# A decoder layer's down projection: where VectorE's queue has the weight sums of steps two and three of a block product, against the residual sums of the product before

## The chip, the cores and the metric

The kernel runs on one core of a Trainium2 chip, in one launch. The metric is device time in microseconds, as the median of several runs. TensorE (PE in the profile) multiplies, VectorE (DVE) and ScalarE (ACT) do the elementwise work, GpSimd (POOL) a few small powers, and SyncE (SP) issues all loads and stores. Each engine works through its own queue in a fixed order, and waits at an instruction whose input isn't there yet.

## The reference

One layer of a decoder trunk on x of 1024 tokens by 1024, all in float32: RMSNorm, one input projection, gated DeltaNet and dilated attention side by side, output projection, residual; then RMSNorm, an up projection to 2 x 2816 columns, a causal convolution of width 3, SiLU gate, the down projection, residual and a last RMSNorm. The part that matters here:

```python
    x = x + jnp.concatenate([o_a, o_b], axis=-1) @ w_out
    h = rmsnorm(x, norm2_w)
    u = causal_dwconv(h @ w_up, ffn_conv_w)
    gate, up = u[..., :D_FF], u[..., D_FF:]
    x = x + (jax.nn.silu(gate) * up) @ w_down          # 2816 -> 1024
    return rmsnorm(x, final_norm_w)
```

## The kernel before

Everything is held transposed: features on the 128 partitions, tokens along the free dimension. A float32 product is made of three fast ones (`mm3`, line 196): each operand is split into a hi part, a rounded copy that ScalarE makes, and a lo part, source minus hi, that VectorE makes (`split_block`, line 1138); the products are hi by hi, hi by lo and lo by hi, in this order.

The down projection (`mlp_down`, line 1452) is a block scheme with seven products instead of eight: the 1024 outputs are halved (512 each, four tiles of 128), the 1024 tokens are halved, and the 2816 inputs are halved (11 tiles of 128 each). It has four stages. Stages 0, 1 and 2 make two block products at a time, one in the four PSUM banks `pa`, one in the four banks `pb`; stage 3 makes one. I call what a stage makes its product. Each stage runs over 11 steps j, called (stage, j) below. A step has, for each of the eight banks, three products of 128 by 128 by 512, so 24.

For a step, `prep` (line 1365) loads the weights (`wd`, `wa`) and activations (`r`, `q`, from the parking place `upark`) and makes the combinations that the scheme needs, on VectorE. In stage 1 these are two weight sums, 512 wide (lines 1381 and 1382), and differences of activations (`t2`, and `r` in place); in stage 2 a weight difference, 1024 wide (1391), a weight sum, 512 wide (1392), and a difference of activations. Then everything is split into hi and lo (`pr` tiles). The weight tiles turn in tags of two buffers each (`wst`, `whi`), so the load of step j + 2 has to wait until step j's tile was last read, which is the lo part of its split.

When a stage's last step (j = 10) is through, `add_to` (line 1415) adds each bank to the residual tiles `x1h` on VectorE: eight residual sums a stage, four for `pa` and four for `pb`. The next stage's first products write the same eight banks in the same order, and each has to wait for its bank's sum. After stage 0's second four, `complete` (1419) also squares the rows on ScalarE and adds the squares on VectorE (`rstdB`).

The residual tiles come from memory by `load_x1` (line 1401): eight loads of 256 KB stand at steps (1,1) and (1,3) of the loop.

What sets the order: TensorE's order is that of the program, held by a token (line 189). In the program's order, the preparation of a step stands ahead of the products of the step before it. The order on the other queues is worked out by the framework's scheduler at build time, from a simulated timeline, so it may put a weight sum of a later step ahead of residual sums that the program has earlier. `after(inst, anchor)` (line 185) is a dependency without a semaphore: the scheduler must put `inst` behind `anchor` in the same queue, and nothing is waited for.

In the order before, the first two weight sums of (1,1) and of (1,2) stand ahead of all eight residual sums of stage 0; among the residual sums stand the lo parts of (1,1). In the same way the difference and sum of (2,1) and the difference of (2,2) stand ahead of all residual sums of stage 1.

Of the kernel before, what the change touches and what calls it, by code (L numbers as in the profile page):

```python
# [10 lines left out]
OP = mybir.AluOpType  # L11
# [133 lines left out]
def hybrid_layer(tc, I, out):  # L145
    nc = tc.nc
    wv = Weave()
    ve = Engine(wv, nc.vector, "vector", 0.07, 0.00105)
# [14 lines left out]
    def tile_(pool, shape, dt, name, tag, bufs):  # L163
        return wv.slot(pool.tile(list(shape), dt, name=name, tag=tag, bufs=bufs), tag, bufs)
# [3 lines left out]
    def A(name, tag, dt=F32, shape=(P, 1024)):  # L168
        if tag in TURNS:
            i = turns[tag] = turns.get(tag, -1) + 1  # L170
            tag = TURNS[tag][i % len(TURNS[tag])]
        return tile_(lp, shape, dt, name, tag, SLOTS[tag])
# [12 lines left out]
    def after(inst, anchor, reason="keeps a slot free until it is needed"):  # L185
        tc.add_manual_dep(inst.ins, anchor.ins.name, order, reason=reason)
# [66 lines left out]
    def half(i):  # L253
        return slice(i * 512, i * 512 + 512)
# [17 lines left out]
    for k in range(KT):  # L272
# [30 lines left out]
        else:  # L303
            inst = ve.tensor_tensor(acc, acc, sq, op=OP.add)
# [1002 lines left out]
    def mlp_up():  # L1307
        yield from wv.until("last weights")
        yield from wv.until("proj")
        up_weights(0, ("A12", "S2", "A22", "S3", "S4"))  # L1310
        rest = None
        for n in range(FT):
            if n + 1 < FT:
                load_up(n + 1)
            yield from up(n, rest)
            rest = last["rest"]
            if n + 1 < FT:
                up_weights(n + 1, UORDER)
        prep(0, 0)
        yield from rest()  # L1320
        wv.done.add("up")
# [12 lines left out]
    def raw_tile(name, tag, src, n=2):  # L1334
        t = tile_(wp, [P, n, 512], F32, name, tag, 2)
        sy.dma_start(t, src)
        return t

    def wd_rows(j, mg):
        v = I["wd"].rearrange("(e j p) c -> j p e c", e=2, p=P)  # L1340
        return v[j, :, :, mg * 512:mg * 512 + 512]

    def acts(name, tag, j, hh):
        t = A(name, tag, shape=(P, 2, 512))
        sy.dma_start(t, upark.rearrange("(e j) p t -> j p e t", e=2)[j, :, :, half(hh)])
        return t

    def split_pair(src):
        hi, lo = [], []
        for d in (hi, lo):  # L1350
            d.append(A("pr", PTAGS[pcount[0] % len(PTAGS)], F32R, (P, 2, 512)))
            pcount[0] += 1
        split_block((hi[0], lo[0]), src)
        return [(hi[0][:, i, :], lo[0][:, i, :]) for i in range(2)]

    def split_one(src, tag=None):
        if tag is None:
            tag = PTAGS[pcount[0] % len(PTAGS)]
            pcount[0] += 1
        t = A("pr", tag, F32R, (P, 2, 512))  # L1360
        b = t[:, 0, :], t[:, 1, :]
        split_block(b, src)
        return b

    def prep(stage, j):
        if stage == 0:

            g = raw_tile("wd", ("wst", "whi")[j % 2], wd_rows(j, 0))
            r = R1[j] = acts("r1", R1TAGS[j], j, 0)
            ops[stage, j] = list(zip(split_pair(g), split_pair(r)))  # L1370
            q = R2[j] = A("r2", R2TAGS[j], shape=(P, 2, 512))
            sy.dma_start(q[:, 0, :], upark[j][:, half(1)])
            ve.tensor_tensor(r[:, 0, :], q[:, 0, :], r[:, 0, :], op=OP.subtract)
        elif stage == 1:

            u = raw_tile("wd", "wst", wd_rows(j, 1))
            a = raw_tile("wa", "whi", wd_rows(j, 0)[:, 0:1], 1)
            r, q = R1[j], R2[j]
            sy.dma_start(q[:, 1, :], upark[HT + j][:, half(1)])
            t2 = tile_(wp, [P, 512], F32, "t2", "wlo", 2)  # L1380
            ve.tensor_tensor(u[:, 1, :], u[:, 0, :], u[:, 1, :], op=OP.add)
            ve.tensor_tensor(u[:, 0, :], u[:, 1, :], a[:, 0, :], op=OP.subtract)
            ve.tensor_tensor(t2, q[:, 1, :], r[:, 0, :], op=OP.subtract)
            w = split_pair(u)
            ops[stage, j] = [(w[0], split_one(t2)), (w[1], split_one(r[:, 0, :]))]
            ve.tensor_tensor(r[:, 1, :], r[:, 1, :], t2, op=OP.subtract)
        elif stage == 2:

            g = raw_tile("wd", "wst", wd_rows(j, 0))
            u = raw_tile("wd", "whi", wd_rows(j, 1))  # L1390
            ve.tensor_tensor(g, g, u, op=OP.subtract)
            ve.tensor_tensor(g[:, 1, :], g[:, 0, :], g[:, 1, :], op=OP.add)
            r = R2[j]
            ve.tensor_tensor(r[:, 0, :], r[:, 1, :], r[:, 0, :], op=OP.subtract)
            ops[stage, j] = list(zip(split_pair(g), split_pair(r)))
        else:

            a = raw_tile("wa", ("wst", "whi")[j % 2], wd_rows(j, 1)[:, 1:2], 1)
            ops[stage, j] = [(split_one(a[:, 0, :]), split_one(R1[j][:, 1, :], R2TAGS[j]))]
# [12 lines left out]
    def part(m, hh, sl):  # L1412
        return slice(512 * hh + sl.start, 512 * hh + sl.stop)

    def add_to(pd, m, hh, sl):
        x = x1h[m][:, part(m, hh, sl)]
        ve.tensor_tensor(x, x, pd[:, sl], op=OP.add)

    def complete(m, hh, sl):

# [31 lines left out]
    def mlp_down():  # L1452
# [4 lines left out]
        def down_step(stage, j):  # L1457
            for e, (op, pds) in enumerate(zip(ops[stage, j], (pa, pb))):
                for i in range(4):
                    down(pds[i], i, op, whole, j == 0 and (stage == 0 or (stage, e) == (1, 1)), j == HT - 1)  # L1460
                if j == HT - 1:
                    mg, hh = ADDS[stage][e]
                    for i in range(4):
                        add_to(pds[i], 4 * mg + i, hh, whole)
                        if stage == 0 and e == 1:
                            complete(i, 0, whole)
                        if stage == 2 and e == 1:
                            complete(i, 1, whole)
                    if stage == 2 and e == 1:
                        for i in range(4):  # L1470
                            complete(4 + i, 1, whole)

        for n, (stage, j) in enumerate(STEPS):
            if n + 1 < len(STEPS):
                prep(*STEPS[n + 1])
            if n in XLOADS:
                load_x1(*XLOADS[n])
            if stage == 3 and j == HT - LAST - 1:
                final_norm(1, whole, ("hf", "ch"), lambda: down_step(stage, j))
            elif stage < 3 or j < HT - LAST:  # L1480
                down_step(stage, j)

        def last_product(i, sl):
            for j in range(HT - LAST, HT):
                down(pa[i], i, ops[3, j][0], sl, False, j == HT - 1)
            add_to(pa[i], 4 + i, 0, sl)
            complete(4 + i, 0, sl)
# [82 lines left out]
```

## Time and profile before

| what | us |
|---|---|
| median of 3 runs | 1223.47 |
| lowest and highest of them | 1223.26, 1225.77 |
| the profiled execution, its own time | 1226.47 |
| its span, first to last instruction | 1224.7 |
| down projection, first product to last residual sum | about 995 to 1206 |

The profile is of one execution. Its times count from the start of the span. A row of an engine's order of time has start, duration, engine, line, operation, what is written and read, the count of merged instructions, and in brackets the idle time before it with what ended it. Since a helper records each operation, nearly all rows have line 139 or 189, and the tile's name tells them apart: `dw` are the eight banks, `x1h<-x1h,dw` a residual sum, `wd<-wd` or `wd<-wd,wa` a weight sum, `pr<-wd`, `pr<-t`, `pr<-r` a hi part on ACT and a lo part on DVE.

### The profile page before, as it was taken

The numbers are of one execution on the slowest core, as the hardware profiler recorded it, in microseconds if no ns is written. First come the engines' busy times: TensorE is split into PE (matmuls) and PEld (weight loads), VectorE is DVE, ScalarE is ACT, GpSimd is POOL, SyncE is SP. The second block draws the span as 40 slices with busy tenths as digits, with TensorE's granted clock in tenths as the row PEclk, the third lists the DMA queues.
The fourth block names the chain that finished last, engine by engine and source line by source line (L and its number), as shares of the span: only waits on it lengthen the run. The fifth ranks groups of instructions, "written<-read, shape, count | busy, mean of one in ns | idle before, by whom it ended". The sixth has DMA issues, their size and how long they took to land.

```text
span 1224.7 us, 18240 instructions
## 1 busy us (share of the span) xinstructions
PE 1203.8 (98%) x7064; PEld 988.3 (81%) x7064; DVE 949.1 (77%) x1458; ACT 574.5 (47%) x1123; POOL 52.1 (4%) x46
## 2 busy tenths in 40 slices
PE   9999999999999999999999999999999999999996
PEld 7878887888777778788788888888888888787886
DVE  7675964566477686767888988889888889899975
ACT  7393344356344453655544444445444544344441
POOL 0211010003100000000000000000000000000000
PEclk9999999999999999999999999999999999999999
DMA  7425252345634213444223122131231497455623
GB/s 231 105 81 161 86 143 82 121 131 154 224 103 123 79 36 118 151 153 138 68 71 103 53 102 89 67 104 59 97 97 59 137 370 240 163 164 175 196 86 138
DMA packets 85800, 154.81 MB, mean 126 GB/s; under 512 B 21169, under 2 KB 36305, under 8 KB 85713
## 3 DMA queue, kind: packets, MB, share of 16 engines
q1 hardware_dynamic: 85712, 153.64, 39.1%
q8 instruction: 55, 0.90, 0.3%
q14 instruction: 33, 0.26, 0.1%
HBM read 117.68 MB, written 35.93 MB: 125 GB/s over the span
## 4 chain that ended last, share of the span: by engine, by line
PE 82%; DVE 7%; DMA 6%; issue 2%; ACT 2%; SPq 0%; POOLq 0%; POOL 0%; DVEq 0%; ACTq 0%
PE ps L189 43%; PE pa L189 19%; PE pc L189 9%; PE dw L189 8%; DMA wd<-in_wd 3%; PE ps L193 3%; DMA r<-upark 2%; DVE pr L139 2%; DVE x1h L139 1%; DVE kT L139 1%; DVE wd L139 1%; PE warm L189 1%; ACT dec L139 1%; DVE wlo L139 0%; DMA wst<-in_wu 0%
## 5 line engine op out<-in xcount | busy, mean ns | idle before, releaser
L189 PE MATMUL dw<-pr 128*128 128x512 f32 (+1 forms) x984 | 213.5, 377 | 3.9 <-DVE x1h L139 3.6
L189 PEld LDWEIGHTS dw<-pr 128*128 128x128 f32 x984 | 176.0, 188 | 40.2 <-DVE x1h L139 4.9
L189 PE MATMUL ps<-xhi,whi 128*128 128x512 f32 x384 | 158.6, 413 | 0.0
L189 PE MATMUL ps<-xhi,wlo 128*128 128x512 f32 x384 | 150.2, 391 | 0.0
L189 PE MATMUL ps<-xlo,whi 128*128 128x512 f32 x384 | 150.0, 391 | 0.0
L189 PE MATMUL pa<-T,pair 128*128 128x512 f32 x528 | 128.7, 393 | 1.2 <-ACT u L139 1.2
L189 PEld LDWEIGHTS pa<-T,pair 128*128 128x128 f32 x528 | 100.1, 190 | 22.4 <-ACT u L139 1.5
L189 PEld LDWEIGHTS ps<-xhi,wlo 128*128 128x128 f32 x384 | 72.1, 188 | 15.7
L189 PEld LDWEIGHTS ps<-xhi,whi 128*128 128x128 f32 x384 | 72.3, 188 | 14.9 <-issue 1.4
L189 PEld LDWEIGHTS ps<-xlo,whi 128*128 128x128 f32 x384 | 72.4, 189 | 11.7
L139 ACT ACTIVATE whi<-wst 128x1024 fp32r<-128x1024 f32 (+2 forms) x42 | 43.0, 1023 | 78.3 <-PE ps L189 64.3
L139 ACT ACTIVATE u<-pa 128x512 f32<-128x512 f32 x44 | 26.3, 598 | 110.7 <-PE pa L189 110.7
L139 DVE SCALAR_TENSOR_TENSOR y<-xu,fcw,y 128x1023 f32<-128x1023 f32 (+1 forms) x44 | 56.3, 1281 | 25.7 <-ACT y L139 25.6
L189 PE MATMUL pc<-B,pair 128*128 128x512 f32 x264 | 63.4, 389 | 0.0
L189 PE MATMUL pa<-B,A 128*128 128x512 f32 x264 | 63.4, 389 | 0.0
L189 PE MATMUL pc<-T,S 128*128 128x512 f32 x264 | 63.4, 389 | 0.0
L189 PE MATMUL pa<-T,S 128*128 128x512 f32 x264 | 63.4, 389 | 0.0
L139 DVE TENSOR_TENSOR wst<-wst 128x512 f32<-128x512 f32 x88 | 60.4, 686 | 0.8
L139 ACT ACTIVATE pr<-wd 128x1024 fp32r<-128x1024 f32 x33 | 34.9, 1059 | 55.1 <-DVE wd L139 35.4
L189 PE MATMUL ps<-B,pair 128*128 128x512 f32 x252 | 60.5, 389 | 0.0
L139 DVE TENSOR_TENSOR wlo<-wst,whi 128x1024 fp32r<-128x1024 f32 (+2 forms) x42 | 49.4, 1177 | 13.8 <-ACT whi L139 13.6
L189 PEld LDWEIGHTS pa<-B,A 128*128 128x128 f32 x264 | 49.6, 188 | 10.3
(240 smaller groups left out, 2343.0 us busy)
## 6 DMA issues: line engine op xcount, KB each, us to landing
wst<-in_wu SPq DMA_DIRECT2D x44, 512.0 KB, 3.7
wd<-in_wd SPq DMA_DIRECT2D x44, 512.0 KB, 4.2
upark<-y SPq DMA_DIRECT2D x22, 512.0 KB, 3.7
wst<-in_wi SPq DMA_DIRECT2D x21, 512.0 KB, 3.7
r<-upark SPq DMA_DIRECT2D x11, 512.0 KB, 8.0
r<-upark SPq DMA_DIRECT2D x22, 256.0 KB, 6.8
wa<-in_wd SPq DMA_DIRECT2D x22, 256.0 KB, 2.8
wst<-in_wv SPq DMA_DIRECT2D x8, 512.0 KB, 3.6
```

Of the source, the lines that this page charges most:

```text
L139: return getattr(eng, op)(*a, **kw)
L189: tc.stamp_issue_order_token(nc.tensor.matmul(dst, lhs, rhs, start=start, stop=stop, **kw).ins, TOKEN)
L193: tc.stamp_issue_order_token(nc.tensor.transpose(dst, src, ident if idt is None else idt).ins, TOKEN)
```

## The change

The weight sums of four steps are put behind certain residual sums of the stage before. The residual sums are collected in a list as they are made, eight a stage. The two weight sums of step (1,1) come behind the fourth residual sum of stage 0, those of (1,2) behind the sixth; those of (2,1) behind the second of stage 1, those of (2,2) behind the sixth. Nothing else is edited; the scheduler then works out all queues anew, so VectorE's, ScalarE's and SyncE's orders differ through the rest of the down projection. TensorE's and GpSimd's are the same.

```diff
+    added = []
+    BEHIND = {(1, 1): 3, (1, 2): 5, (2, 1): 1, (2, 2): 5}
+
+    def behind(stage, j, insts):
+        if (stage, j) in BEHIND:
+            for inst in insts:
+                after(inst, added[8 * (stage - 1) + BEHIND[stage, j]], "the banks of the stage are added first")
+
     def prep(stage, j):
...
-            ve.tensor_tensor(u[:, 1, :], u[:, 0, :], u[:, 1, :], op=OP.add)
-            ve.tensor_tensor(u[:, 0, :], u[:, 1, :], a[:, 0, :], op=OP.subtract)
+            behind(stage, j, [ve.tensor_tensor(u[:, 1, :], u[:, 0, :], u[:, 1, :], op=OP.add),
+                              ve.tensor_tensor(u[:, 0, :], u[:, 1, :], a[:, 0, :], op=OP.subtract)])
...
-            ve.tensor_tensor(g, g, u, op=OP.subtract)
-            ve.tensor_tensor(g[:, 1, :], g[:, 0, :], g[:, 1, :], op=OP.add)
+            behind(stage, j, [ve.tensor_tensor(g, g, u, op=OP.subtract),
+                              ve.tensor_tensor(g[:, 1, :], g[:, 0, :], g[:, 1, :], op=OP.add)])
...
     def add_to(pd, m, hh, sl):
         x = x1h[m][:, part(m, hh, sl)]
-        ve.tensor_tensor(x, x, pd[:, sl], op=OP.add)
+        added.append(ve.tensor_tensor(x, x, pd[:, sl], op=OP.add))
```

## The prediction

> **What bounds the kernel now.** I read the page first, then a table of stretches around the down projection, then TensorE's order of time there, and then what VectorE, ScalarE and the loads did at the stops.
>
> ```profile
> span 1224.7 us, 18240 instructions
> PE 1203.8 (98%) x7064; PEld 988.3 (81%) x7064; DVE 949.1 (77%) x1458; ACT 574.5 (47%) x1123; POOL 52.1 (4%) x46
> PE 82%; DVE 7%; DMA 6%; issue 2%; ACT 2%; SPq 0%; POOLq 0%; POOL 0%; DVEq 0%; ACTq 0%
> wd<-in_wd SPq DMA_DIRECT2D x44, 512.0 KB, 4.2
> ```
>
> TensorE has work for 98% of the span and carries 82% of the chain that ended last: only time in which it stands still can be won. The stretches (us, then busy us of PE, PEld, DVE, ACT, POOL, granted clock, DMA share, GB/s) show where that is:
>
> ```profile
> 1052.00:1063.00 11.00, 9.91 (x41) 7.23 (x41) 10.86 (x17) 4.30 (x7) 0.00 (x0) 1.00 0.56 178
> 1063.00:1115.00 52.00, 52.00 (x232) 43.02 (x231) 46.32 (x66) 20.34 (x28) 0.00 (x0) 1.00 0.56 180
> 1115.00:1126.00 11.00, 8.47 (x35) 6.10 (x34) 11.00 (x16) 4.64 (x5) 0.00 (x0) 1.00 0.47 147
> 1205.00:1225.00 20.00, 9.40 (x75) 8.69 (x73) 11.41 (x30) 2.26 (x6) 1.39 (x2) 0.84 0.38 127
> ```
>
> The two short stretches are the passages from product 0 to 1 and from 1 to 2. There VectorE is full and TensorE is not; in between TensorE never stops. TensorE's own order of time gives the stops:
>
> ```profile
> 978.60 2.72 PE pa L189 x12
> 1011.80 44.95 PE L189 MATMUL dw<-pr 128*128 128x512 f32 x197 [0.25 <-DVE pr L139]
> 1057.02 0.96 PE L189 MATMUL dw<-pr 128*128 128x512 f32 x3 [0.27 <-DVE x1h L139]
> 1058.22 3.01 PE L189 MATMUL dw<-pr 128*128 128x512 f32 x12 [0.24 <-DVE x1h L139]
> 1061.82 8.46 PE L189 MATMUL dw<-pr 128*128 128x512 f32 x36 [0.59 <-DVE x1h L139]
> 1069.66 47.53 PE L189 MATMUL dw<-pr 128*128 128x512 f32 x209
> 1118.09 2.33 PE L189 MATMUL dw<-pr 128*128 128x512 f32 x9 [0.89 <-DVE x1h L139]
> 1121.53 3.00 PE L189 MATMUL dw<-pr 128*128 128x512 f32 x12 [1.11 <-DVE x1h L139]
> 1125.05 68.98 PE L189 MATMUL dw<-pr 128*128 128x512 f32 x303 [0.53 <-DVE x1h L139]
> L189 PE MATMUL dw<-pr 128*128 128x512 f32 x864 | 198.4, 390 | 3.9 <-DVE x1h L139 3.6 <-DVE pr L139 0.2
> ```
>
> All six stops are ended by residual sums (x1h). The printed idle times are too small: twelve products take 2.72 (0.227 each), but a product is drawn 0.39 long, so the next could start 0.16 before the printed end. From start to start: the first run ends at 1056.75, the next product could start at 1056.59 and starts at 1057.02 (0.43); three products later 1057.70, started 1058.22 (0.52); twelve later 1060.94, started 1061.82 (0.88): **1.83** lost. In the same way 1117.03 to 1118.09 (1.06), 1120.13 to 1121.53 (1.40), 1124.25 to 1125.05 (0.80): **3.26**. Together 5.1 us, 0.42% of the span, is all that there is to win.
>
> What VectorE does at the first passage, with ScalarE's hi parts and SyncE's loads:
>
> ```profile
> 1049.77 0.63 ACT L139 ACTIVATE pr<-r 128x512 fp32r<-128x512 f32 x1 [3.86 <-PE dw L189]
> 1050.31 1.04 ACT L139 ACTIVATE pr<-wd 128x1024 fp32r<-128x1024 f32 x1
> 1052.14 0.69 DVE L139 TENSOR_TENSOR wd<-wd 128x512 f32<-128x512 f32 x1 [2.23 <-DMA wd<-in_wd]
> 1053.96 1.28 DVE L139 TENSOR_TENSOR x1h<-x1h,dw 128x512 f32<-128x512 f32 x2
> 1055.15 1.22 DVE L139 TENSOR_TENSOR pr<-wd,pr 128x1024 fp32r<-128x1024 f32 x1
> 1056.29 0.68 DVE L139 TENSOR_TENSOR x1h<-x1h,dw 128x512 f32<-128x512 f32 x1
> 1056.40 0.38 SPq L139 DMA_DIRECT2D wd<-in_wd  x1
> 1056.87 4.28 SPq L139 DMA_DIRECT2D x1h<-xpark  x8
> 1057.49 2.47 DVE L139 TENSOR_TENSOR x1h<-x1h,dw 128x512 f32<-128x512 f32 x4
> 1061.68 1.21 DVE L139 TENSOR_TENSOR pr<-wd,pr 128x1024 fp32r<-128x1024 f32 x1
> 1071.47 0.68 DVE L139 TENSOR_TENSOR pr<-t,pr 128x512 fp32r<-128x512 f32 x1
> ```
>
> Four sums take 2.47, so one takes 0.60 of the queue (the last is drawn 0.68); a 1024-wide one 1.14 (1055.15 to 1056.29). The first weight sum of step (1,2) waits 2.23 for its load, and the residual sums wait behind it although the banks are ready: product 1 begins at 1056.59 - 2 x 0.68 = 1055.23 (the two sums at 1053.96 had freed two banks, the third, at 1056.29, ended the stop), so the ended product's first bank was complete 7 x 0.68 earlier, at 1050.5 (1050.6 with the 0.16).
>
> **The change, part by part.** No instruction is added or removed. In the changed program VectorE's order at passage 0-1 is: four residual sums, first weight sum of (1,1), two residual sums, first sum of (1,2), second sum of (1,1), two residual sums, second sum of (1,2), then the lo parts. At 1-2: two residual sums, difference (2,1), a lo part, two, sum (2,1), two, difference (2,2), two, lo parts.
>
> **Stops that go at passage 0-1.** The lo part ahead of the sums needs ScalarE's hi part (1049.77 + 0.63), so it runs at 1050.4; residual sums from 1051.0 at 0.60, each behind its bank, weight sums between: the eighth is done at 1057.7. TensorE wants that bank at 1055.23 + 7 x 0.68 = 1060.0. All 1.83 goes, with 2.3 to spare.
>
> **What is late next there.** The second sum of (1,1) now ends at 1056.5, so ScalarE's hi part (1.04; it was at 1050.31) ends at 1057.6. VectorE has the lo part of (1,1) at 1058.8 to 1060.1 (it was 1055.15 to 1056.4) and the operand's lo part done at 1060.7. TensorE, no longer held, wants it for the second product of (1,1), 1055.23 + 5.44 + 0.23 = 1060.9: 0.2 to spare, cost nothing.
> The weight tiles have two buffers, so the load of (1,3), at 1056.40 before, can only start at 1060.1. Behind it SyncE now has six x1h loads (eight before), then the load of (1,4), whose buffer the lo part of (1,2) frees at 1063.0 as before (1061.68 + 1.21). And VectorE's queue has the first sum of (1,4) ahead of the lo part of (1,3), as it had before.
>
> ```profile
> 1041.72 3.58 DMA wd<-in_wd
> 1062.92 6.17 DMA wd<-in_wd
> 1108.42 5.27 DMA wd<-in_wd
> GB/s 295 383 386 398 387 375 260 287 179 86 86 128 124 371 107 130 174 143 157 217 155 263 179 87 193 230 183 226 199 146 111 131 169 4 0 46 299 62 110 173
> ```
>
> These are pieces of the chain (start, us from issue to landing) and the GB/s of 40 slices from 980 on. An unhindered load takes 3.58; a full queue moves 398 GB/s, 0.66 for 256 KB and 1.32 for 512 KB. So (1,3) lands at 1063.7, six loads later it is 1067.6, (1,4) at 1069.0. The same sum for before gives 1060.0 + 5.3 + 1.3 = 1066.6, but that load landed at 1069.1, 2.5 later. So 1069.0 to 1071.5. From there VectorE needs the first sum 0.60, lo (1,3) 1.14, the second sum 0.60, the operand's lo 0.68 and hops, 3.1: ready at 1072.1 to 1074.6. TensorE wants it at 1055.23 + 3 x 5.44 + 0.23 = 1071.8. (Before: ready at 1071.47 + 0.68, wanted 1.83 later than now, 1.5 to spare.) New stop **0.3 to 2.8**; I take the middle, 1.6, as nothing says which share of those 2.5 returns.
>
> **Stops that go at passage 1-2.**
>
> ```profile
> 1111.32 1.22 DVE L139 TENSOR_TENSOR pr<-r,pr 128x1024 fp32r<-128x1024 f32 x1
> 1113.78 1.23 DVE L139 TENSOR_TENSOR wd<-wd 128x1024 f32<-128x1024 f32 x1 [1.24 <-DMA wd<-in_wd]
> 1117.26 1.87 DVE L139 TENSOR_TENSOR x1h<-x1h,dw 128x512 f32<-128x512 f32 x3
> ```
>
> Product 2 begins at 1117.03; the first bank is complete at 1112.4, yet its sum starts at 1117.26 because weight sums, one of them waiting for a load, stand ahead. In the new order two sums run from 1112.5, the difference (2,1) at 1113.7, and the eighth sum ends at 1120.9, against 1121.8 wanted: 3.26 goes. New: lo parts of (2,1) follow, 1.14 and 1.22, to 1123.2, wanted at 1117.03 + 5.44 + 0.23 = 1122.7: **0.5**. Then the difference (2,3) stands ahead of the lo part of (2,2), and its load waits for the lo part of (2,1), done at 1122.0. It lands 3.58 to 5.27 later; then 1.14 + 1.14 + 0.60 + 1.22 = 4.1: 1129.7 to 1131.4, wanted at 1122.7 + 0.5 + 5.44 = 1128.6. Stop **1.1 to 2.8**; with the page's median of 4.2, 1.7.
>
> **VectorE's lateness.** At passage 1-2 it has no slack: 1111.32 + 1.22 = 1112.5 meets the first bank at 1112.4. The lo part of (1,1) is now 3.7 late, and each load hangs on a lo part two steps earlier, so lateness is handed on. Against it: of 52 us between the passages VectorE is busy 46.3, so 5.7 is spare, part of it waiting for loads. What remains at passage 1-2 is between 0 and 3.7, and delays all eight sums and their weight sums alike; I take half, **1.9**.
>
> **The sum.** -1.8 + 1.6 - 3.3 + 0.5 + 1.7 + 1.9 = **+0.6 us**. The profiled execution took 1226.47 (its span 1224.7 and 1.77 around it), so it would become 1227.1; it was 3.0 longer than the median of the runs, 1223.47, and I carry the difference over: **1224.1**.
>
> A rule to weigh: the Trainium skill, "DMA: Bandwidth & Descriptors", section "Anatomy of one DMA", gives about 2.0 us plus bytes over 436 GB/s, for 512 KB an estimate of 3.2 us. By it the stop at (2,2) would be 0.7 and the sum 1.0 lower; that section fits another issuing path, and the loads here (3.58 at best) speak against it.
>
> **Rivals.** *Late weights win (slower).* The weight chain load, sum, hi, lo is now the last to arrive. With (1,4) landing at 1071.5 and 3.7 late at passage 1-2: 2.8 + 0.5 + 1.7 + 3.7 - 5.1 = +3.6, **1227.1**. It turns slower by more than 0.2% (2.45 us, about what a measurement can tell from no change) once the new stops pass 7.5. For it: the two buffers and 2.5 us of unexplained landing time; against it: 5.7 spare on VectorE.
> *The sums win (faster).* The lateness is made up by passage 1-2 and loads land unhindered: 0.3 + 0.5 + 1.1 - 5.1 = -3.2, **1220.3**. For it: the first stops surely go; against it: the median wd load takes 4.2, not 3.58.
> *The clock falls (slower).* In the last stretch TensorE is busy 9.4 of 20 us and the granted clock is 0.84, 3.2 us of clock missing; in the passages, with stops up to 1.4, it stays at 1.00. A single stop of 2.8 at (1,3) might bring such a fall: 0.6 + 3.2 = +3.8, **1227.3**. The Trainium skill, "TensorE: Matmul & The Clock Gate", section "Why this matters for your kernels", warns of stops over some 3 us; the rows above agree as far as they go.
> *Nothing moves.* Were the order left as it was: 1223.5; but the built order differs.
>
> **How the numbers follow.** Forecast 0.50, late weights 0.31, clock 0.03, sums 0.14, nothing moves 0.02. So faster 0.14, same 0.52, slower 0.34. The forecast's own terms reach from -3.2 to +4.7; cutting about a tenth at each end leaves 1221.0 to 1227.3.
>
> **What would show it.** Right: no x1h behind the waits of dw at either passage; a stop at (1,3), near 1072, and at (2,1) and (2,2), near 1123 and 1129, ended by lo parts (pr); the load of (1,3) issued near 1060. Wrong: the stretch 1063 to 1115 without a stop, so that the 1.83 is kept; x1h stops still there at passage 1-2, so that VectorE came late by more than I took.

## The result, and the profile after

The changed kernel took **1227.77 us** (median of 8 runs, 1225.34 to 1229.96), the kernel before 1224.32 in the same comparison (8 runs, 1223.26 to 1225.77). The ratio is **1.0024**, with a 95% interval of 1.0015 to 1.0033: slower by 2.9 us, 1.8 to 4.0 (the two medians are 3.45 apart; the interval holds both). On the 1223.47 that the forecast started from, that is 1226.4: inside its range (1221.0 to 1227.3), above its 1224.1, and near the rival of the late weights (1227.1). The profiled execution took 1226.66, which is 1.1 under the median of its kernel; that of before took 1226.47, which is 2.1 over. So two such pages show less of the difference than the runs do.

The page of the changed kernel, its span, engines and chain:

```profile
span 1224.9 us, 18235 instructions
PE 1202.0 (98%) x7064; PEld 986.2 (81%) x7064; DVE 949.8 (78%) x1458; ACT 574.0 (47%) x1123; POOL 50.6 (4%) x46
PE 82%; DVE 9%; DMA 4%; issue 3%; ACT 2%; POOL 0%; SPq 0%; POOLq 0%; DVEq 0%; ACTq 0%
```

TensorE still carries 82% of the chain; VectorE and issue (time in which an engine waited for nothing that the profile shows) have gained where DMA has lost. The same stretches as before (us, then busy us of PE, PEld, DVE, ACT, POOL, granted clock, DMA share, GB/s), with the one behind the second passage added:

```profile
1052.00:1063.00 11.00, 11.00 (x50) 9.07 (x49) 11.00 (x17) 6.37 (x10) 0.00 (x0) 1.00 0.45 134
1063.00:1115.00 52.00, 50.83 (x225) 41.74 (x224) 44.48 (x64) 19.70 (x27) 0.00 (x0) 1.00 0.60 192
1115.00:1126.00 11.00, 8.82 (x35) 6.04 (x34) 10.12 (x14) 4.12 (x5) 0.00 (x0) 1.00 0.48 154
1126.00:1205.00 79.00, 77.94 (x378) 65.34 (x378) 63.76 (x83) 33.92 (x48) 1.01 (x1) 1.00 0.45 149
```

The first passage is full now (11.00 of 11, it was 9.91). The 52 us between the passages, full before, have lost 1.17; the second passage has won only 0.35; and the stretch behind it, full before (79.00 of 79), has 1.06 of idle time. TensorE's order of time in the changed kernel says who ended each stop:

```profile
993.32 16.71 PE L189 MATMUL dw<-pr 128*128 128x512 f32 x73
1010.18 60.17 PE L189 MATMUL dw<-pr 128*128 128x512 f32 x264 [0.15 <-DVE pr L139]
1071.52 44.99 PE L189 MATMUL dw<-pr 128*128 128x512 f32 x197 [1.17 <-DVE pr L139]
1116.88 3.44 PE L189 MATMUL dw<-pr 128*128 128x512 f32 x12 [0.37 <-DVE x1h L139]
1121.01 1.88 PE L189 MATMUL dw<-pr 128*128 128x512 f32 x7 [0.69 <-DVE x1h L139]
1123.88 5.75 PE L189 MATMUL dw<-pr 128*128 128x512 f32 x24 [0.99 <-DVE pr L139]
1130.37 22.05 PE L189 MATMUL dw<-pr 128*128 128x512 f32 x96 [0.74 <-DVE pr L139]
1152.75 40.87 PE L189 MATMUL dw<-pr 128*128 128x512 f32 x179 [0.32 <-DVE pr L139]
```

This down projection starts at 993.32, 1.43 earlier than in the profile of before, so every time here is compared with 1.43 taken off. In the order of the rows: no stop at all where the residual sums (x1h) had held TensorE at 1057 to 1062; a stop at step (1,3), ended by a lo part (pr); two stops at the second passage still ended by x1h; lo parts again at (2,1), (2,2) and, not foreseen, (2,6). From start to start, counted as in the prediction, they are 1.33, 0.53, 1.41 (1116.88 + 12 x 0.227 = 1119.60, next at 1121.01), 1.28, 1.05 and 0.49: 6.1 us of stops where the profile of before had 5.1. The stretch from the first product of the down projection to the last norm's first product is 200.14 long, and was 199.11: +1.0, which the stops account for.

VectorE's order of time in the changed kernel, at the first passage and at (1,3), then at the second passage:

```profile
1054.81 1.28 DVE L139 TENSOR_TENSOR x1h<-x1h,dw 128x512 f32<-128x512 f32 x2
1057.21 1.23 DVE L139 TENSOR_TENSOR pr<-wd,pr 128x1024 fp32r<-128x1024 f32 x1
...
1068.44 0.69 DVE L139 TENSOR_TENSOR wd<-wd 128x512 f32<-128x512 f32 x1 [1.65 <-DMA wd<-in_wd]
1069.05 1.22 DVE L139 TENSOR_TENSOR pr<-wd,pr 128x1024 fp32r<-128x1024 f32 x1
...
1070.78 0.69 DVE L139 TENSOR_TENSOR pr<-t,pr 128x512 fp32r<-128x512 f32 x1
...
1098.26 0.69 DVE L139 TENSOR_TENSOR wd<-wd 128x512 f32<-128x512 f32 x1 [0.54 <-DMA wd<-in_wd]
1100.73 1.22 DVE L139 TENSOR_TENSOR pr<-wd,pr 128x1024 fp32r<-128x1024 f32 x1
1107.32 1.23 DVE L139 TENSOR_TENSOR wd<-wd 128x1024 f32<-128x1024 f32 x1 [2.42 <-DMA wd<-in_wd]
1113.21 1.28 DVE L139 TENSOR_TENSOR x1h<-x1h,dw 128x512 f32<-128x512 f32 x2
```

The eighth residual sum of stage 0 is done at 1054.81 + 2 x 0.60 = 1056.0. At 1068.44 the first weight sum of (1,4) comes after a wait of 1.65 for its load, and the lo part of (1,3), which needed nothing more, stands behind it; the lo part of 1070.78 ends at 1071.47 and releases TensorE at 1071.52. Near the second passage the same figure is seen on a larger scale: a sum that waits for its load (1098.26), the lo part of (1,9) behind it (1100.73), the load of (2,0) that needs the buffer of (1,9), the difference of (2,0) that waits 2.42 for it, and the residual sums at 1113.21. SyncE's rows, and the loads in the chain of the changed kernel (start, us from issue to landing):

```profile
1058.46 0.38 SPq L139 DMA_DIRECT2D wd<-in_wd  x1
1058.93 2.90 SPq L139 DMA_DIRECT2D x1h<-xpark  x6
1061.92 0.60 SPq L139 DMA_DIRECT2D wd<-in_wd  x1
```
```profile
1061.92 6.49 DMA wd<-in_wd
1101.99 5.21 DMA wd<-in_wd
1122.72 3.41 DMA wd<-in_wd
```

### The profile page after: what moved, and what is told of

Its sections match the earlier page's. It is cut to its first block, busy times and chain, and to the rows that moved or that the text cites. A ratio compares the mean times of both kernels' runs of the same rounds, so it can differ in the third digit from the quotient of the medians.

```text
span 1224.9 us, 18235 instructions
## 1 busy us (share of the span) xinstructions
PE 1202.0 (98%) x7064; PEld 986.2 (81%) x7064; DVE 949.8 (78%) x1458; ACT 574.0 (47%) x1123; POOL 50.6 (4%) x46
## 4 chain that ended last, share of the span: by engine, by line
PE 82%; DVE 9%; DMA 4%; issue 3%; ACT 2%; POOL 0%; SPq 0%; POOLq 0%; DVEq 0%; ACTq 0%
PE ps L189 43%; PE pa L189 19%; PE pc L189 10%; PE dw L189 8%; PE ps L193 3%; DMA wd<-in_wd 3%; DVE pr L139 2%; DVE wd L139 1%; DVE x1h L139 1%; DVE kT L139 1%; ACT dec L139 1%; DMA xt<-in_xT 1%; DVE wlo L139 0%; DMA wst<-in_wu 0%; ACT pr L139 0%
## 5 line engine op out<-in xcount | busy, mean ns | idle before, releaser
L139 DVE TENSOR_TENSOR wst<-wst 128x512 f32<-128x512 f32 x88 | 60.4, 687 | 0.8
```

The source lines that it names most:

```text
L139: return getattr(eng, op)(*a, **kw)
```

## The experiments

Two questions were open: which of the new stops carry the loss, and whether it comes from the four moves themselves or from the order that the scheduler then gave to the steps behind them. Ratios are against the kernel before, run between the others on the same chip; they are not the quotients of two medians. The first four kernels were run in one comparison, the next two in a second, the last four in a third, and each comparison had its own chip.

| kernel | median us | ratio | 95% interval |
|---|---|---|---|
| first passage's part only | 1225.92 | 1.0015 | 1.0006 to 1.0024 |
| second passage's part only | 1223.54 | 0.9996 | 0.9987 to 1.0004 |
| change, lo parts ahead | 1223.59 | 0.9989 | 0.9981 to 0.9998 |
| change, x1h loads later | 1225.68 | 1.0016 | 1.0007 to 1.0024 |
| lo parts ahead, without the change | 1223.27 | 0.9990 | 0.9981 to 0.9999 |
| first part, one lo part ahead | 1222.89 | 0.9996 | 0.9987 to 1.0005 |
| moves only, other order as before | 1224.19 | 1.0000 | 0.9991 to 1.0009 |
| changed kernel's order, one swap | 1226.67 | 1.0015 | 1.0006 to 1.0023 |
| changed kernel's order, two swaps | 1227.09 | 1.0019 | 1.0010 to 1.0027 |
| moves and swaps, other order as before | 1223.77 | 0.9997 | 0.9989 to 1.0006 |

### One passage at a time

```diff
-    BEHIND = {(1, 1): 3, (1, 2): 5, (2, 1): 1, (2, 2): 5}
+    BEHIND = {(1, 1): 3, (1, 2): 5}       # first part only
+    BEHIND = {(2, 1): 1, (2, 2): 5}       # second part only
```

> Only the weight sums of (1,1) and (1,2) are put behind residual sums; stage 2's stay as before. Theory (late weights): the stops at passage 0-1 (1.8 us from start to start) go, one stop of 1 to 3 us at (1,3) near 1072 comes, ended by a lo part (pr); passage 1-2 keeps its stops ended by x1h (3.3). Time within -1 to +2 us of before. Rival (the loss is not in the down projection): +2 to +3 us as with the whole change, without stops that account for it. Rival (the second passage makes the loss): no change from before.

> Only the weight sums of (2,1) and (2,2) are put behind residual sums; stage 1's stay as before. Theory: passage 0-1 keeps its 1.8 us of x1h stops, there is no stop at (1,3); at passage 1-2 the x1h stops (3.3) go and stops ended by lo parts come at (2,1) and (2,2), 1 to 3 us together. Time -2 to 0 us against before. Rival (the loss is not in the down projection): +2 to +3 us. Rival (the second passage makes the loss): +2 us or more.

The first part alone costs 1.0015, the second alone nothing that can be told (0.9996). TensorE's rows of the second part alone:

```profile
1056.52 3.02 PE L189 MATMUL dw<-pr 128*128 128x512 f32 x12 [0.24 <-DVE x1h L139]
1060.11 66.56 PE L189 MATMUL dw<-pr 128*128 128x512 f32 x292 [0.57 <-DVE x1h L139]
1127.48 22.09 PE L189 MATMUL dw<-pr 128*128 128x512 f32 x96 [0.81 <-DVE pr L139]
```

Here the second passage has no stop by x1h: 66.56 us run through it, up to the stop of (2,2). So the stops by x1h that the changed kernel has there come with the first part. What this pair can't tell is how: by lateness handed on, or by another order of the steps in between, since the scheduler orders them anew for each kernel. The first part alone brings both: up to the second passage VectorE's operations stand there in the changed kernel's order, and SyncE's loads do so throughout.

### The lo parts ahead of the next sum, by two further dependencies

```diff
+            if j == 3:
+                LOWS[1, 4] = lows[-3:-1]   # sums of (1,4) behind lo parts of (1,3)
...
+            if j == 2:
+                LOWS[2, 3] = lows[-2:]     # sums of (2,3) behind lo parts of (2,2)
```

In the first of these kernels the whole change is kept; the second keeps none of it (`BEHIND = {}`); the third has the first passage's part and the order at (1,4) alone.

> The whole change, and two more orders of the same kind: the weight sums of (1,4) come behind the lo parts of (1,3), those of (2,3) behind the lo parts of (2,2). Theory (a weight sum that waits for its load stands ahead of the lo part that TensorE needs): the stop at (1,3) goes (1.3 from start to start in the changed kernel's profile) and the one at (2,2) too (0.9); a smaller stop may come a step later. Time 1.5 to 4 us under the changed kernel, at or under before. Rival (the load of (1,3) itself, started later, is what is late): the stop at (1,3) stays, time as the changed kernel. Rival (not in the down projection): as the changed kernel.

> The kernel before with only the two orders of e3 that put the weight sums of (1,4) behind the lo parts of (1,3) and those of (2,3) behind the lo parts of (2,2); no weight sum is put behind residual sums. Theory (e3 gains because the lo parts, which the changed order made late, are brought forward, and so the x1h stops of the kernel before are free to go): without the change's own part the x1h stops of passage 0-1 stay at 1.8 us and those of 1-2 at 1 to 3, ended by x1h; time -2 to +0.5 us against before, and above e3. Rival (the two new orders alone make e3's gain, whatever stands around the residual sums): time as e3, 1 us or more under before, with few x1h stops.

> e1 (only stage 1's weight sums behind residual sums) and the one order that puts the weight sums of (1,4) behind the lo parts of (1,3). Theory: e1's stop at (1,3), 1.4 from start to start, goes and at most 0.8 comes a step later; the x1h stops at passage 1-2 stay; time 1 to 2.5 us under e1, about before. Rival (the stop at (1,3) comes from the late load, not from VectorE's order): the stop stays over 1 us and the time is e1's.

TensorE's rows with the whole change and both orders:

```profile
1012.89 109.25 PE L189 MATMUL dw<-pr 128*128 128x512 f32 x480 [0.22 <-DVE pr L139]
1123.03 68.11 PE L189 MATMUL dw<-pr 128*128 128x512 f32 x299 [0.89 <-DVE pr L139]
```

TensorE runs 109 us through the first passage, (1,3) and the second passage's banks; one stop is left, at (2,1). The ratio is 0.9989: 3.5 permille or 4.3 us under the changed kernel, where the two stops of (1,3) and (2,2) that the two orders aim at are 1.33 + 1.05. Without the change the same two orders give 0.9990, so the change itself adds nothing to them that these runs can tell. In the profiles of these two the stretch is 196.17 and 196.57 long, the shortest of all. In the third kernel the stop went from (1,3) to (1,4):

```profile
1079.41 40.27 PE L189 MATMUL dw<-pr 128*128 128x512 f32 x176 [1.22 <-DVE pr L139]
```

and still its time fell from 1.0015 to 0.9996. Gains larger than the stop that was removed, and a gain where a stop only moved, say that these dependencies change more than the place that they name. They do: the scheduler places the other instructions of the down projection anew as well. So these three don't isolate what they were meant to, and the last four kernels were made for that.

### The residual tiles' loads later

```diff
-    XLOADS = {6: (0, 0), 12: (1, 0), 14: (0, 1), 16: (1, 1)}
+    XLOADS = {6: (0, 0), 14: (0, 1), 17: (1, 0), 19: (1, 1)}
```

> The whole change, with the eight x1h loads of the second half of the outputs moved five and three steps later in the program, so that none stands between the loads of (1,3) and (1,4). Theory's second part (the queue of x1h loads makes the load of (1,4) land late, 6.5 us after issue in the changed kernel): that load lands in 3.6 to 4.5 us, the stop at (1,3) shrinks to under 0.3, the stops of passage 1-2 stay or grow; time 0 to 2 us under the changed kernel. Rival (VectorE's order alone): the stop at (1,3) stays at 1 us or more.

TensorE's rows with the x1h loads away from the load of (1,4):

```profile
1093.14 25.93 PE L189 MATMUL dw<-pr 128*128 128x512 f32 x113 [1.24 <-DVE pr L139]
1120.09 1.88 PE L189 MATMUL dw<-pr 128*128 128x512 f32 x7 [1.02 <-DVE x1h L139]
1123.56 68.11 PE L189 MATMUL dw<-pr 128*128 128x512 f32 x299 [1.59 <-DVE pr L139]
```
```profile
1065.30 0.69 DVE L139 TENSOR_TENSOR wd<-wd 128x512 f32<-128x512 f32 x1
1067.76 1.23 DVE L139 TENSOR_TENSOR pr<-wd,pr 128x1024 fp32r<-128x1024 f32 x1
```

The stop at (1,3) is gone. VectorE still has the first sum of (1,4) (1065.30) ahead of the lo part of (1,3) (1067.76), but the sum no longer waits for its load, so those loads did make the load of (1,4) late. A stop came behind the place where they now stand (1093.14), the stops by x1h and at (2,1) stayed, and 1.0016 is left.

### Each kernel once more

> The kernel before, profiled once more. Theory (the whole loss is made between the first product of the down projection and the last stop, and the first profile of before was one of its longer executions): the stretch from the first dw product to the first product of the last norm is shorter than the 199.1 us of the first profile, by 1 to 2, with smaller x1h stops. Rival (the first two profiles are typical and 2 us of the loss are made elsewhere): 199 us again.

> The changed kernel, profiled once more. Theory: the same stretch takes 200 to 203 us, with the stops at (1,3), (2,1) and (2,2) ended by lo parts, and what lies ahead of it is as in before. Rival (2 us of the loss are made elsewhere): the stretch takes 200 us and the time ahead of it is 1 to 2 us longer than in before.

No edit. The kernel before, in a second execution (1225.0 us), TensorE's rows:

```profile
1011.29 46.00 PE L189 MATMUL dw<-pr 128*128 128x512 f32 x200 [0.24 <-DVE pr L139]
1057.53 3.01 PE L189 MATMUL dw<-pr 128*128 128x512 f32 x12 [0.23 <-DVE x1h L139]
1061.12 57.53 PE L189 MATMUL dw<-pr 128*128 128x512 f32 x252 [0.59 <-DVE x1h L139]
1119.78 3.03 PE L189 MATMUL dw<-pr 128*128 128x512 f32 x12 [1.13 <-DVE x1h L139]
1123.31 69.02 PE L189 MATMUL dw<-pr 128*128 128x512 f32 x303 [0.50 <-DVE x1h L139]
```

Four stops instead of six, of 0.40, 0.87, 1.29 and 0.81 from start to start: 3.4 us where the first profile had 5.1. The stretch is 197.99, and was 199.11; that is 1.1 less and not 1.7, since a row also runs over stops too short to be printed. The changed kernel again (1225.65) has 199.39 (200 to 203 was expected), after 200.14, with the same stops at (1,3), at the passage, at (2,1) and (2,2). The second part alone, whose order up to the second passage is that of before, has the smaller stops at the first passage too (0.40 and 0.87). The means, 198.55 and 199.77, are 1.2 apart; two executions of one kernel differ by nearly as much.

### VectorE's order written out

In these four kernels 148 VectorE instructions, from the first passage to stage 3, are tied each to the one before it, in a list, so that the scheduler has no say in that queue. ScalarE's and SyncE's orders still are the scheduler's. SyncE's in the kernel with one swap is the changed kernel's, in the moves only it is that of the kernel before, but for the loads of (1,2) and (1,4), which stand earlier.

```diff
+    queue = [wv.made["I-" + i] for i in ORDER.split()]
+    for first_, then in zip(queue, queue[1:]):
+        after(then, first_, "VectorE's order is written out")
```

"Moves only" takes the two passages from the changed kernel's order and all else in the relative order of the kernel before. The kernels with swaps start from the changed kernel's list: one swap puts the first sum of (1,4) behind two lo parts of (1,3), two swaps put the two sums of (2,3) behind the lo parts of (2,2) as well. The last one has both swaps in the list of the moves only.

> VectorE's order in the down projection is written out in full here: the two passages as in the changed kernel, everything between and behind them in the relative order of the kernel before, so that the moves are there without the scheduler's new order of the later steps. Theory 'the moves cost it' (weight sums behind residual sums make the weight chain late): as the whole change, 1.0015 to 1.003, with stops of about 1.3 at (1,3) and 0.9 at (2,2). Theory 'the new order costs it' (the scheduler's order of the steps behind the passages, with two weight sums in a row ahead of a lo part, as at step (2,6)): at or under the kernel before, 0.9990 to 1.0005, and no stop at (2,6).

> The changed kernel's order of VectorE written out, with one instruction moved: the first weight sum of (1,4) behind two lo parts of (1,3). Loads are as in the changed kernel. Theory 'a sum that waits for its load stands in the way of a ready lo part': the stop of 1.3 at (1,3) goes and the ratio falls by about 1.1 permille, to 1.0013. Theory 'the load of (1,4) is late anyway': the stop moves to (1,4), as in the kernel with the first passage's part and this order, and the ratio stays at 1.0020 to 1.0030.

> As the kernel with one swap, with the difference and the sum of (2,3) also behind the lo parts of (2,2). Theory 'a sum that waits for its load stands in the way': the stops at (1,3) and (2,2), 1.3 and 0.9, both go: 1.0024 less 1.8 permille, 1.0006. Theory 'the scheduler's new order made most of the gain of the kernel with the lo parts ahead (0.9989)': it stays above 1.0012, since nothing else is moved here.

> The moves alone, with both swaps, everything else in the order of the kernel before: the candidate for the best version. If the moves and the two sums ahead of lo parts are all that counts, at most 0.9990, with stops of under 2 us together at the passages. If the order behind the passages counts, near 1.0000.

The moves only take 1.0000 (0.9991 to 1.0009): the moves in themselves cost nothing that can be told. Against the changed kernel that is 2.4 permille less, 2.9 us give or take 1.6 (two intervals of 0.9 permille each, added in squares). The kernels that keep the changed kernel's order behind the passages, run in the same comparison as the moves only, take 1.0015 and 1.0019. The profiles agree: the stretch is 197.77 and 197.75 long in the two kernels with the old order behind the passages, and 199.02 to 200.18 in the four profiles with the changed kernel's order. So the loss goes with the new order, and the theory that the moves make it falls. The new order is VectorE's together with the loads and hi parts that go with it; which engine's part of it costs was not separated.

TensorE's rows of the moves only:

```profile
1072.21 5.73 PE L207 MATMUL dw<-pr 128*128 128x512 f32 x24 [1.43 <-DVE pr L139]
1078.65 43.82 PE L207 MATMUL dw<-pr 128*128 128x512 f32 x192 [0.71 <-DVE pr L139]
1123.44 68.11 PE L207 MATMUL dw<-pr 128*128 128x512 f32 x299 [0.97 <-DVE pr L139]
```

Not one stop is ended by x1h, at either passage. The weight chain has its stops at (1,3), (1,4) and (2,1), 1.60, 1.00 and 1.13 from start to start: 3.7 us. Nothing comes behind 1123.44, where the changed kernel has (2,2) and (2,6). VectorE's rows at its second passage:

```profile
1105.19 1.22 DVE L139 TENSOR_TENSOR wd<-wd 128x1024 f32<-128x1024 f32 x1
1112.09 1.37 DVE L139 TENSOR_TENSOR x1h<-x1h,dw 128x512 f32<-128x512 f32 x2 [0.31 <-PE dw L207]
```

The difference of (2,0) waits for no load (2.42 in the changed kernel), and the first residual sum now waits for TensorE. TensorE had lost 1.3 more by then than in the changed kernel, so the bank itself came later here. In the changed kernel it was complete at about 1112.09 less those 1.3 and the 0.30 by which its down projection started earlier, 1110.5, and its sum started at 1113.21, 2.7 late. Counted from the first product of the down projection, VectorE is free for that sum 118.2 us on in the moves only (1112.09 - 0.31 - 993.62), and 119.9 in the changed kernel: the order makes 1.7 of those 2.7. It is already there at the lo part of (1,9), 105.7 against 107.4:

```profile
1099.36 1.22 DVE L139 TENSOR_TENSOR pr<-wd,pr 128x1024 fp32r<-128x1024 f32 x1
```

By an estimate from the same figures, the other 1.0 would be there with the moves alone too, had TensorE not been held 1.3 longer.

The chain of waits between 1060 and 1160, for the changed kernel, for the moves only, and for the changed kernel in its second execution:

```profile
by line: DMA wd<-in_wd 32.0%; DVE pr L139 20.5%; DVE wd L139 14.2%; issue 13.0%; PE dw L189 7.3%; DVE x1h L139 4.9%; ACT pr L139 4.3%; DVE r L139 2.0%; DVE t L139 1.9%; DVEq L139 0.2%; ACTq L139 0.1%
```
```profile
by line: PE dw L207 70.0%; DMA wd<-in_wd 9.5%; DVE pr L139 7.2%; DVE wd L139 5.3%; DVE x1h L139 4.1%; issue 2.2%; DVE r L139 2.0%; DVE rstdB L139 1.1%; DVE t L139 0.6%; DVEq L139 0.0%
```
```profile
by line: PE dw L189 57.2%; DMA wd<-in_wd 15.2%; DVE pr L139 8.7%; DVE wd L139 7.9%; DVE x1h L139 4.9%; issue 4.3%; ACT pr L139 1.1%; DVE r L139 0.7%; DVEq L139 0.1%; ACTq L139 0.0%
```

In the changed kernel's first profile TensorE holds 7.3% of that chain: for 100 us the time is set by load, sum, hi part, lo part and the next load. With the moves alone it holds 70.0%, but in the second execution of the changed kernel it holds 57.2%, and in the kernel before 35.0%. So this share tells which chain came last in one execution; it doesn't measure what an order costs.

The swaps say what a single place is worth. One swap leaves 1.0015, two leave 1.0019, both near the changed kernel's 1.0024 and far from the 0.9989 of the kernel in which the scheduler was free. TensorE's rows with one swap, then with two:

```profile
1011.55 105.00 PE L207 MATMUL dw<-pr 128*128 128x512 f32 x461 [0.22 <-DVE pr L139]
```
```profile
1123.84 16.62 PE L207 MATMUL dw<-pr 128*128 128x512 f32 x72 [1.00 <-DVE pr L139]
1140.95 11.22 PE L207 MATMUL dw<-pr 128*128 128x512 f32 x48 [0.49 <-DVE pr L139]
```

One swap does remove the stop at (1,3), without its coming back at (1,4), and its ratio is 0.9 permille lower, as expected of a 1.3 us stop (though the intervals overlap). The second swap removes the stop of (2,2), a smaller one comes at (2,4), and nothing is won that the runs can tell. With the old order behind the passages both swaps bring 0.9997, not told apart from 1.0000 without them.

## Why the prediction went as it did

*What bounds the kernel.* Right, but the size was that of one execution: 5.1 us of stops, against 3.4 in a second profile of the same program. **This is the first step that failed**: "it was 3.0 longer than the median of the runs, 1223.47, and I carry the difference over". Part of that excess was the very stops that the change removes (1.7 of it by the rows of the second profile, 1.1 by the length of the stretch), so there was less to win in a common execution than in the one at hand. With 4.25, the mean of both, the forecast's own terms give 1.6 + 0.5 + 1.7 + 1.9 - 4.25 = +1.45 instead of +0.6; by the length of the stretch it would be about +1.2. Two profiles are few to say what is common.

*Stops that go at passage 0-1.* Right: all of them. The eighth sum was forecast for 1057.7, 1056.3 with the 1.43 taken off, and was done at 1056.0.

*New stop at (1,3).* Right in place, mechanism and size: 1.33 and 1.28 in the two profiles, forecast 1.6 in 0.3 to 2.8. The load of (1,3) was issued at 1058.46 (forecast 1060.1 - 1.43 = 1058.7); the load of (1,4) landed at 1068.41 (forecast 1067.6 to 1070.1).

*(2,1) and (2,2).* Right in place and mechanism. The sum is right by luck: 1.28 and 1.05 were measured, 0.5 and 1.7 forecast, and the two errors cancel. The load of (2,3) took 3.41, not the 4.2 that was taken. (The shortest of the 44 loads in the profile of before took 3.5, so 3.58 was not the best.) The stop of 0.49 at (2,6) was not foreseen: two differences in a row stand there ahead of a lo part.

*VectorE's lateness.* Right in size by luck, 0.53 + 1.41 = 1.9 of stops by x1h at the second passage where half of 3.7 was taken, and **wrong in its cause, the second step that failed**. It was put down to the lo part of (1,1), "3.7 late", and lateness that "is handed on". In the changed kernel itself that lateness all but goes and comes anew. Counted from the first product of the down projection, the lo part of (1,1) is 3.5 late (63.9, and 60.4 before); that of (1,3), two steps on, 0.8 (75.7, from 1069.05, and 75.0 before, from the row below); that of (1,9) 2.4 (107.4, and 105.1 before).

```profile
1069.73 1.22 DVE L139 TENSOR_TENSOR pr<-wd,pr 128x1024 fp32r<-128x1024 f32 x1
```

The kernel with the moves only has the lo part of (1,1) nearly as late (63.3) and the same two buffers, but that of (1,9) at 105.7, and VectorE is free 1.7 us earlier at the second passage. So most of what is late there is made between the passages, by the new order; the rows above show sums that wait for their loads ahead of lo parts that free buffers. The prediction read that order at (1,4) and (2,3) and not in the steps around them.

*The sum.* In the pair of profiles that it was made from, +0.6 was forecast and +1.0 found. Four profiles give +1.2, the runs +2.9 (1.8 to 4.0). The differences among profiles of one kernel, 1.1 and 0.75, are of the order of the gap that remains, so they don't settle it, and its cause stays open; the profiled executions of before happened to be long ones (1226.47 and 1225.0 against a median of 1224.32), those of the changed kernel short ones (1226.66 and 1225.65 against 1227.77).

*Rivals.* "Late weights win" has the right side and, by the runs, nearly the right time; but its stops were to pass 7.5 us and were 6.1, and 4.5 by the rows of the second profile. The measured 0.24% (0.15 to 0.33) came with fewer stops than that, and the lateness was not the one that it started from. "The sums win" fell with the stops at the second passage. The clock stayed at 1.00 in every stretch shown between 1052 and 1205. The order did change.

## What to carry to other kernels

When a scheduler works out a queue anew, a small edit changes the whole queue: here the edit itself cost nothing that could be told (1.0000) and the new order behind it 2.4 permille, give or take 1.3. An experiment on such a kernel has to write the order out; those that left the scheduler free gave gains that the place they named could not explain. And a stop that is to be won should be sized in more than one execution: the rows of the same program show 5.1 and 3.4 us of them. The share of a chain of waits changes as much: 7.3% and 57.2% for TensorE in two executions of one kernel.

The best versions that were run are the two with lo parts ahead and the scheduler free, 0.9990 (0.9981 to 0.9999) and 0.9989 (0.9981 to 0.9998): 1.2 and 1.3 us under the kernel before, less than the 0.2% that the prediction took for telling a difference, and not told apart from the four kernels at 0.9996 to 1.0000. Which part of their order brings it was not isolated.

## What the runs showed of the hardware

VectorE's and TensorE's orders ahead of the down projection are the same in all these kernels, yet its first product comes at 993.02 to 995.32 in the fourteen profiles (994.75 and 994.18 before, 993.32 and 993.35 after the change): a spread of 2.3 us that the change has no part in. Even a single stop printed as long as 1.59, ahead of 1123.56 in the kernel with the x1h loads later, left the granted clock of its stretch at 1.00:

```profile
1115.00:1126.00 11.00, 8.39 (x35) 6.25 (x35) 10.43 (x14) 4.54 (x5) 0.00 (x0) 1.00 0.45 147
```
